# Moving the wait for the last stores from SP, ahead of the closing barriers, to ACT, behind them

## Chip, cores, metric

One core of one Trainium2 chip. Its engines are called PE (TensorE), ACT (ScalarE), DVE (VectorE), POOL (GpSimd) and SP (SyncE). The metric is device microseconds of one execution. Where two kernels are compared, they ran in alternation on the same chip.

## The reference

Max-unpooling: each of 16 x 64 images of 32 x 32 floats is spread over a 64 x 64 image; an index of 0 to 3 says into which of the four places of a 2 x 2 block a value goes, and the other three are zero.

```python
out_i = i * kernel_size + idx // kernel_size
out_j = j * kernel_size + idx % kernel_size
output[b, c, out_i, out_j] = x[b, c, i, j]
```

It reads 4 MB of values and 8 MB of indices (64-bit, of which the low halves are used) and writes 16 MB.

## The kernel before

Three loads are issued ahead of the opening barrier. DVE makes the output in four groups, each from operations "index equals p, times x". SP stores each group, 4 MB, once DVE has made it. The semaphore `stored` counts the last three stores, 16 for each.

```python
class Program:                      # writes the kernel's instructions into the first block
    def __init__(self, nc):
        self.nc = nc
        self.block = nc.main_func.blocks[0]
    ...
        for g in range(NG):         # NG = 4
            nc.sync.wait_ge(made, g + 1)
            nc.sync.dma_start(out=out_v[g], in_=out_t[g]).then_inc(
                stored if g else stored_0, 16
            )
        nc.sync.sem_inc(made, -NG)                                    # L143
        nc.sync.wait_ge(stored, 16 * (NG - 1)).then_inc(stored, -16 * (NG - 1))   # L144
```

Leaving the framework's context (L175) adds the closing code, in a block of its own: a drain of SP, then two barriers of all five engines. (A drain waits for the engine's own work: in this trace DVE's starts at 41.628 us and ends at 55.515, just after DVE's last operation, which ends at 55.467.) In one barrier each of PE, ACT, DVE and SP drains and counts up one semaphore; POOL waits for four counts and releases the four. Behind the program stands what the runtime adds: a chain that each engine has to join, then the clearing of semaphores, then a second chain. In the trace a chain is nine counts of one semaphore; a hop is the time from one count to the next, and an engine's way is the time from the end of its last instruction to its count.

## Time and profile before

| | before |
|---|---|
| time, median of 4 (lowest to highest) | 72.69 us (72.57 to 72.78) |
| span, first to last instruction of the program | 71.00 us |
| last store's last count lands | 70.309 us |
| SP's wait for it is over | 70.343 us |
| last closing instruction (PE) ends | 71.002 us |
| runtime's first chain: first to ninth count | 71.236 to 71.761 us |
| runtime's second chain: ninth count | 72.906 us |

Times inside a run count from the first instruction of the program. "The landing" is the last of the 48 counts of `stored`: with it the last three stores are done. The lower five rows are single records of the trace, which the page does not list: sequencer instructions and the times at which semaphores change. The prediction was written when the kernel before had three runs with a median of 72.71 us.

### The profile page before, as it was taken

What the parts mean: (1) busy time and instruction counts of PE and PEld (TensorE: products, weight loads), DVE (VectorE), ACT (ScalarE), POOL (GpSimd) and SP (SyncE); (2) the same over time, 40 slices, a digit from 0 to 9 for tenths busy, and PEclk for the clock granted to TensorE, in tenths of its full rate; (3) what the DMA queues carried; (4) which work ended last, traced back from release to release, by engine and by line L of the source; (5) the groups of instructions that cost most, each with busy time, mean ns of one, the idle gap of its engine ahead of it and who ended that gap; (6) DMA issues with size and microseconds to landing.
All of it is one profiled execution on the core that took longest, in us unless ns stands there. A gap on an engine that the chain in (4) does not pass through costs nothing.

```text
span 71.0 us, 72 instructions
## 1 busy us (share of the span) xinstructions
DVE 35.6 (50%) x20; POOL 0.2 (0%) x4
## 2 busy tenths in 40 slices
DVE  0000000000089999999999999999999200000000
POOL 1000000000000000000000000000000000000000
DMA  9598997998988999879696989899898979696980
GB/s 277 240 434 378 517 498 314 443 462 378 563 369 369 462 577 438 369 314 572 295 591 295 517 369 517 369 425 462 369 517 351 535 314 572 295 591 295 517 369 0
DMA packets 1009, 29.36 MB, mean 414 GB/s; under 512 B 113, under 2 KB 113, under 8 KB 113
## 3 DMA queue, kind: packets, MB, share of 16 engines
q1 hardware_dynamic: 864, 26.21, 86.4%
q10 hardware_dynamic: 144, 3.15, 10.3%
q14 instruction: 1, 0.00, 0.0%
HBM read 12.58 MB, written 16.78 MB: 414 GB/s over the span
## 4 chain that ended last, share of the span: by engine, by line
DVE 45%; DVEq 4%; issue 1%
DVE out_t L127 45%; DVEq L175 4%
## 5 line engine op out<-in xcount | busy, mean ns | idle before, releaser
L127 DVE SCALAR_TENSOR_TENSOR out_t<-idx_t,x_t 128x2048 f32<-128x2048 int32 (+1 forms) x20 | 35.6, 1860 | 19.9 <-DVEq L116 19.9
L161 POOL MEMSET const-bfloat16-1.0<- 128x1 bf16 x1 | 0.1, 103 | 0.0
L161 POOL MEMSET const-uint8-127<- 128x1 uint8 x1 | 0.1, 102 | 0.0
L161 POOL MEMSET const-float32-1.0<- 128x1 f32 x1 | 0.1, 100 | 0.0
L161 POOL MEMSET const-float32-0.0<- 128x1 f32 x1 | 0.1, 99 | 0.2 <-issue 0.2
## 6 DMA issues: line engine op xcount, KB each, us to landing
out_dram<-out_t SPq DMA_DIRECT2D x4, 4096.0 KB, 13.5
idx_t<-in_indices_dram SPq DMA_DIRECT2D x1, 5120.0 KB, 31.2
x_t<-in_x_dram SPq DMA_DIRECT2D x1, 4096.0 KB, 19.5
idx_t<-in_indices_dram ACTq DMA_DIRECT2D x1, 3072.0 KB, 19.6
```

Of the source, the lines that this page charges most:

```text
L127: op = nc.vector.scalar_tensor_tensor(out=o_c[:, k : k + n, :, pidx // 2, :, pidx % 2], in0=idx_c[:, t : t + n], scalar=pidx, in1=x_c[:, t ...
L161: nc = _bacc.Bacc("TRN2", target_bir_lowering=False, num_devices=1)
L175: with _tile.TileContext(nc) as tc:
```

## The change

Its intent: let the closing barriers run while the stores are still under way, and let one engine alone, ACT, hold up the end until the stores have landed. ACT does nothing else at that time.

```diff
+    def last(self, made):
+        def move(nc):
+            ins = self.block.instructions
+            at = next(k for k, i in enumerate(ins) if i.name == made.ins.name)
+            nc.main_func.blocks[-1].instructions.append(ins.pop(at))
+        self.nc.at_finalize(move)
 ...
         nc.sync.sem_inc(made, -NG)
-        nc.sync.wait_ge(stored, 16 * (NG - 1)).then_inc(stored, -16 * (NG - 1))
+        program.last(
+            nc.scalar.wait_ge(stored, 16 * (NG - 1)).then_inc(stored, -16 * (NG - 1))
+        )
```

`last` takes the instruction out of its place when the program is finished and puts it behind everything else.

## The prediction

> **What bounds the kernel now.** I read the page first, for what was busy to the end; then the chain that ended last; then the SP queue's own waits; then stretches of the tail; and last the single sequencer records of the last microsecond.
>
> ```profile
> span 71.0 us, 72 instructions
> DVE 35.6 (50%) x20; POOL 0.2 (0%) x4
> DVE  0000000000089999999999999999999200000000
> DMA  9598997998988999879696989899898979696980
> HBM read 12.58 MB, written 16.78 MB: 414 GB/s over the span
> out_dram<-out_t SPq DMA_DIRECT2D x4, 4096.0 KB, 13.5
> ```
>
> The DMA row is busy from the first slice to the last but one: 29.36 MB in 71 us. DVE works only in the middle half. So the kernel is bound by its traffic: loads, then four stores of 4 MB. The chain that ended last shows only compute, and so stops early:
>
> ```profile
> 19.79 0.08 issue
> 19.87 11.82 DVE out_t L127 x7
> ...
> 41.63 2.83 DVEq L175
> 44.46 11.01 DVE out_t L127 x5
> ```
>
> It ends at 44.46 + 11.01 = 55.47 us, and 15.5 us of the span are left. (The "DVEq L175" in it is DVE's closing drain, fetched early and held behind its own operations; it is no stop.) What fills the rest is in the SP queue's waits:
>
> ```profile
> SPq L140 <- DVE out_t L127: 53.2, 4, 27.6
> SPq L144 <- SPq L144: 14.5, 1, 14.5
> SPq L175 <- PEq L175: 0.4, 2, 0.3
> ```
>
> L144 is the wait that the change moves. SP sits in it for 14.5 us, until the last three stores have landed. L175 is the closing code, and there are 0.4 us of waits of SP in it. The stretches say what the machine does then:
>
> ```profile
> core 0: us, DVE busy (x) POOL busy (x), PEclk, DMA share, GB/s
> ...
> 55.30:70.30 15.00, 0.17 (x1) 0.00 (x0) 1.00 0.91 393
> 70.30:71.00 0.70, 0.00 (x0) 0.00 (x0) 1.00 0.00 0
> ```
>
> Up to 70.3 us the stores run. In the last 0.7 us no byte moves and no engine computes. That stretch is what the change is about. By the records of the two lines concerned it is all semaphore work:
>
> ```profile
> L144 SPq EVENT_SEMAPHORE  x1: 17/17/17, 70.3 to 70.3; - x1
> ...
> L175 POOLq EVENT_SEMAPHORE  x4: 17/17/17, 70.5 to 70.9; - x4
> L175 SPq DRAIN  x3: 7/7/7, 70.4 to 70.7; - x3
> ...
> L175 ACTq EVENT_SEMAPHORE  x2: 17/17/17, 70.6 to 70.9; - x2
> ...
> L175 PEldq EVENT_SEMAPHORE  x2: 51/51/51, 70.6 to 71.0; - x2
> ```
>
> The single records (us from the span's start): the last 32 KB store packet ends at 69.951; its 16th count lands at 70.309; SP's wait runs 70.326 to 70.343; SP drains at 70.404 and 70.459; POOL sees four arrivals at 70.491 and releases at 70.570; the four others pass at 70.611 to 70.674. A second barrier of the same kind follows: drains from 70.651, PE's the last at 70.774; POOL sees all at 70.819, releases at 70.897; SP, ACT (ends 70.960), DVE and PE pass, PE last, 70.951 to 71.002. From the end of the wait to the end of the span: 71.002 - 70.343 = 0.659 us.
>
> **What the Trainium skill says.** "Perfetto Trace Analysis", section "Summary: the profiler window per engine type": a sequencer instruction is shown for its execution alone, and its wait is hidden. The trace agrees: L144 lasts 17 ns although SP waited 14.5 us. "DMA: Bandwidth & Descriptors", section on the anatomy of one DMA: a semaphore is only counted up once the last byte is confirmed. Here the last count comes 70.309 - 69.951 = 0.36 us after the last data packet. The change keeps that. "Runtime: NRT & Kernel Launch", section "The ~15µs preamble/postamble breakdown": behind the program stands the runtime's own barrier of all engines, a chain over five engines with some 44 ns a hop, then the clearing of semaphores, then another barrier. The trace has them: nine counts of one semaphore at 71.236, 71.271, 71.476, 71.520, 71.543, 71.641, 71.681, 71.715 and 71.761; clears of semaphores from 71.661 to 72.325; nine counts more, 72.549 to 72.906. So hops are 23 to 98 ns here, but one took 205 ns.
>
> **The change, part by part.**
> (1) Removed: SP's wait ahead of its closing drain. SP's last other work, taking `made` back, ends at 55.89. SP then reaches the closing barriers at once. DVE's drain ended at 55.515 and ACT, PE and POOL have been there since 1.3 us. So both barriers run at about 55.9 to 56.6, under the stores, some 13.7 us before they can matter. Their 0.659 us leave the path.
> (2) Added: the same wait as the last instruction of ACT, behind both barriers. The list of the built program confirms it: ACT's wait for 48 is the very last instruction; nothing else moves (the comparison of instruction orders shows shifted line numbers only). Cost: 17 ns on ACT as on SP, since every event instruction of ACT and SP is 17 ns. So ACT ends at 70.34, and I expect a **span of 70.34 us**.
> (3) Unmoved: issues, DVE's work and transfers. The stores land at 70.31 as before.
> (4) Behind the span: the runtime's barrier used to start once all five had come out of the second closing barrier, PE last at 71.002. Now four engines stand in it for 14 us and only ACT is missing. Which place ACT has in the chain the trace does not name. If it is second (its count at 71.271, 0.311 after its own end at 70.960), the second count comes at 70.343 plus at most 0.311, thus by 70.654, and the rest goes at the pace of the undisturbed opening chain, where the seven hops from the second count to the ninth took 38+43+24+112+39+34+46 = 336 ns: over by 70.99 instead of 71.761, a gain of at least 0.77. With only 0.1 us for ACT's way there it would be 0.98. If ACT is the third, the late one, its way is 71.476 - 70.960 = 0.516 and the gain 71.761 - (70.343 + 0.516 + 0.298) = 0.60; as fifth (count at 71.543, way at most 0.583, then 0.231) at least 0.60. Reading the clears by their blocks of numbers, I take the order to be PE, ACT, POOL, DVE, SP: ACT second. The late third is then POOL, which has long been there after the change.
> Sum: 0.659 from the span, plus about 0.15 of the runtime's chain that is waited out earlier: **some 0.8 us**. The profiled run took 72.79 for a span of 71.00, so the metric holds 1.79 us beside the span, and I take it that the first runtime barrier is inside that. 72.71 - 0.8 = **71.9 us**, 1.1% less.
>
> **The rivals.**
> (a) **Span only.** The runtime's part does not shrink, or it is outside the metric: 72.71 - 0.66 = 72.05. For it: 1.79 us beside the span are not itemised by any view. Against: the late hop of 205 ns is waiting, and can be hidden.
> (b) **Nothing gained.** Whatever the metric ends on waits for something other than the five engines, for example a slower way out of ACT after a long wait, or work in the closing that POOL or SP does only once stores are done: 72.7. For it: on several engines the way from the last instruction to the runtime's chain is up to 0.5 us, and unseen. Against: that way was paid before too, after the barriers.
> (c) **The whole tail goes**, and with it more of the runtime's closing: engines that came early might clear their semaphores under the stores. That would save 1.5 us or more: 71.2. Against: the clears start only at 71.661, after the chain has turned round, hence after all arrivals; ACT's missing arrival holds them as before.
> (d) **Slower.** Four engines waiting early could disturb the stores. They move nothing, and SP waited through the same 14.5 us before. Cost 0.
>
> **Range and chances.** The centre is 71.9. The places of ACT in the chain span 0.60 to 0.98, thus 71.73 to 72.11; the runs of before scatter from 72.57 to 72.78, so a median may be off by 0.1. That gives 71.65 to 72.2, with (a) inside and (b) and (c) outside. Faster by over 2% needs a gain of 1.45 us, twice what stands behind the wait: 0.03. Slower by 2% has no mechanism: 0.01. Within 2%: 0.96.
>
> **What will show it.** Right: a span near 70.3; closing-code records (L187) of SP, POOL, DVE and PE near 56 us and none after 57; ACT's event for the stores at 70.3 as the last of all; the stores' landing still about 14.8 us after the last issue; the runtime's chain over by about 71.0 and the clears in the same shape some 0.8 us sooner. Step (2) is wrong if ACT's event lasts much over 17 ns or comes much later than the last count; step (4) is wrong if the profiled time falls by just the span's 0.66, or by less. The whole is wrong if the last store lands later, or if the closing barriers still stand at the end.

## The result

| | time, median (lowest to highest) | ratio to before |
|---|---|---|
| before | 72.69 us (72.57 to 72.78), 4 runs | |
| changed | 71.83 us (71.83 to 71.85), 4 runs | 0.9883 (0.9866 to 0.9901) |

A ratio is the mean time of one kernel's runs over that of the other's of the same rounds, so it is not quite the ratio of the medians quoted; the interval is of 95%. The change gains 1.2%: clear of noise.

The page of the changed kernel:

```profile
span 70.3 us, 72 instructions
DMA  9699998999988899969999896979999997969792
HBM read 12.58 MB, written 16.78 MB: 417 GB/s over the span
```

The traffic is the same, the span is 0.7 us shorter, and the DMA row no longer ends in an idle slice. The chain that ended last still stops with DVE (start, length, what):

```profile
44.37 11.01 DVE out_t L137 x5
```

55.38 us, against 55.47 before: the work was not touched. The SP queue's waits (total, times, longest):

```profile
SPq L150 <- DVE out_t L137: 53.1, 4, 27.5
SPq L187 <- PEq L187: 0.4, 2, 0.3
```

The wait of 14.5 us has gone from SP, while the 0.4 us in the closing code, now L187, are still there. They have moved in time, as the records of the closing code say (durations in ns, then first and last start in us):

```profile
L187 POOLq EVENT_SEMAPHORE  x4: 17/17/17, 56.0 to 56.4; - x4
L187 SPq DRAIN  x3: 7/7/64, 55.9 to 56.2; - x3
...
L187 PEldq EVENT_SEMAPHORE  x2: 51/51/51, 56.1 to 56.5; - x2
```

Before, these stood at 70.4 to 71.0 us. The barriers are as long as they were, but run under the stores. And the moved wait:

```profile
L155 ACTq EVENT_SEMAPHORE  x1: 17/17/17, 70.3 to 70.3; - x1
```

It is the only instruction of the program after 56.6 us. The stretches show the same end:

```profile
55.30:70.30 15.00, 0.08 (x1) 0.00 (x0) 1.00 0.91 393
70.30:70.40 0.10, 0.00 (x0) 0.00 (x0) 1.00 0.00 0
```

The stores run at 393 GB/s in both kernels; barriers and engines waiting beside them do not slow them. What comes after the span is seen in the nine counts of the runtime's first chain (single records, us from the span's start):

```
               landed   1      2      3      4      5      6      7      8      9
before         70.309 71.236 71.271 71.476 71.520 71.543 71.641 71.681 71.715 71.761
changed        70.291 56.755 70.474 70.512 70.555 70.579 70.678 70.716 70.750 70.797
```

In the changed kernel the first count comes at 56.755, 0.234 us after the closing barriers are over, and the second is held for 13.7 us. One engine stands ahead of ACT in the chain, so ACT is the second. The third count follows 38 ns later, not 205. From the landing to the ninth count it takes 70.797 - 70.291 = 0.506 us, against 71.761 - 70.309 = 1.452 before: 0.946 us less. From there to the ninth count of the second chain it is 1.145 and 1.148 us: unchanged. The two profiled runs took 72.79 and 71.83 us, 0.96 apart. The metric thus moves with the runtime's chain, not with the span, which fell by 0.673.

### The profile page after: what moved, and what is told of

Read it like the earlier page. It is cut to its first block, busy times and chain, and to the rows that moved or that the text cites. A ratio compares the mean times of both kernels' runs of the same rounds, so it can differ in the third digit from the quotient of the medians.

```text
span 70.3 us, 72 instructions
## 1 busy us (share of the span) xinstructions
DVE 35.6 (51%) x20; POOL 0.2 (0%) x4
## 4 chain that ended last, share of the span: by engine, by line
DVE 46%; DVEq 4%; issue 1%
DVE out_t L137 46%; DVEq L187 4%
```

## The experiments

One theory and its rivals were left after this. **T:** what counts is the work that still stands between the landing and the ninth count: closing barriers, the engine's way into the chain, and the hops behind its place. **Rivals:** the gain needs ACT in place of SP (E); the place in the chain does not matter (P); barriers cost wherever they stand. Eleven runs, all correct, on three chips. The last column is read from each profiled run, in us.

| run | who waits, and where | median us | ratio to before (95%) | landing to ninth count |
|---|---|---|---|---|
| e1 | ACT, behind both barriers (the change) | 71.71 | 0.9863 (0.9848 to 0.9878) | 0.506 |
| e2 | ACT, ahead of both | 72.65 | 0.9991 (0.9978 to 1.0005) | 1.417 |
| e3 | SP, behind both | 71.55 | 0.9843 (0.9828 to 0.9858) | 0.332 |
| e4 | POOL, behind both | 72.16 | 0.9925 (0.9912 to 0.9938) | 0.887 |
| e5 | SP, between them | 72.34 | 0.9946 (0.9932 to 0.9959) | 1.065 |
| e6 | SP, ahead of three barriers | 73.03 | 1.0038 (1.0025 to 1.0051) | 1.780 |
| e7 | ACT, behind three barriers | 71.71 | 0.9853 (0.9840 to 0.9867) | 0.505 |
| e8 | PE, behind both | 71.95 | 0.9887 (0.9874 to 0.9901) | 0.712 |
| e9 | DVE, behind both | 71.71 | 0.9861 (0.9847 to 0.9876) | 0.473 |
| e10 | SP, behind both, again | 71.59 | 0.9844 (0.9830 to 0.9858) | 0.332 |
| e11 | ACT, behind both, again | 71.72 | 0.9864 (0.9850 to 0.9878) | 0.507 |

The kernel before had 72.68, 72.75 and 72.74 us (e1 to e4, e5 to e8, e9 to e11).

### e1: the changed kernel as yardstick

No edit.

> The changed kernel once more, as the yardstick of this chip for the three that follow. Theory T (what counts is what still stands behind the last store: the 0.66 us of closing barriers have gone under the stores, and the runtime's chain is entered by its second engine, ACT, with 0.47 us left to its ninth count): 71.83 us, 0.85 us under the kernel before; closing-code records near 56 us; the ninth count of the runtime's chain near 70.80. Every rival expects the same here.

71.71 us and 0.9863: a little more gain than at first (0.9883). The trace after the landing is the same to the nanosecond, 0.506 us; the landing itself was earlier, 70.077. The two profiled runs took 71.83 and 71.61 us: 0.22 apart, as their landings are (0.214). So the difference between these two is when the transfers were over, and nothing behind them.

### e2: ACT waits, but where SP did

```diff
-        nc.sync.wait_ge(stored, 16 * (NG - 1)).then_inc(stored, -16 * (NG - 1))
+        nc.scalar.wait_ge(stored, 16 * (NG - 1)).then_inc(stored, -16 * (NG - 1))
```

> ACT waits instead of SP, but ahead of the closing barriers, where SP's wait was. Theory T: both barriers are behind the stores again, so the time is that of the kernel before, 72.69, or at most 0.06 less, as ACT has one closing drain behind its wait where SP has two (61 ns between them in the trace of before). Span near 70.95. Rival E (ACT is the better engine to wait on, wherever it waits): near 71.8.

0.9991, an interval that holds 1. Rival E falls: the engine alone is worth nothing that the time shows. The SP queue's wait tells where the 14.5 us went, with the records of ACT's drains below it:

```profile
SPq L175 <- PEq L175: 14.9, 2, 14.6
```

```profile
L175 ACTq DRAIN  x2: 8/8/8, 70.3 to 70.6; - x2
```

SP now stands in the first closing barrier for 14.6 us, because ACT's drain for it comes at 70.3 and no longer at 1.3 us. (The view names PE as the releaser; the one that came last is ACT.) Landing to ninth count is 1.417 us, 0.035 less than before; I had allowed up to 0.06 for SP's second drain. (The 61 ns of the expectation lie between the end of SP's wait and its first drain; the two drains start 55 ns apart.)

### e3: SP waits, behind the barriers

The edit, against the changed kernel:

```diff
-            nc.scalar.wait_ge(stored, 16 * (NG - 1)).then_inc(stored, -16 * (NG - 1))
+            nc.sync.wait_ge(stored, 16 * (NG - 1)).then_inc(stored, -16 * (NG - 1))
```

> SP keeps the wait, but behind the closing barriers. Theory T with the order PE, ACT, POOL, DVE, SP in the runtime's chain: SP is the turning point, so four counts are in long before and only the fifth to ninth (0.218 us after the fifth) are behind the stores; if SP needs 0.145 us from its last instruction to its count as ACT did, the ninth count is 0.36 us after the wait against ACT's 0.468: 71.73 us. Four counts near 56.8 to 57.1. Rival E (the gain needs ACT): near 72.7. Rival P (the place in the chain does not matter): 71.83.

71.55 us, where 71.73 was expected: the place alone gives the whole gain, and 0.16 us more than ACT's in the medians. In the SP queue's waits the long one is back, and the end is early all the same:

```profile
SPq L155 <- SPq L155: 13.9, 1, 13.9
SPq L187 <- PEq L187: 0.4, 2, 0.3
```

The counts of e3, e4, e8 and e9 together show where each engine stands:

```
               landed   1      2      3      4      5      6      7      8      9
e3 SP          70.160 56.611 56.645 56.850 56.895 70.328 70.372 70.410 70.445 70.492
e4 POOL        70.305 56.778 56.812 70.907 70.950 70.974 71.071 71.111 71.145 71.192
e8 PE          70.283 70.637 70.671 70.709 70.753 70.777 70.875 70.914 70.948 70.995
e9 DVE         70.145 56.628 56.662 56.867 70.376 70.400 70.498 70.537 70.571 70.618
```

With SP four counts are in before the landing, and the fifth is held. With SP as the last to come the sixth count follows the fifth in 44 ns; in the other runs that hop takes 97 to 99. This I had not expected (0.363 us from SP's wait against 0.298 measured, 70.492 - 70.194). Why it is shorter no run here shows. (One reading, untested: in all other runs the sixth count comes 121 to 123 ns after the fourth, which is DVE's by row e9; with SP last the fourth count is 13.4 us old by then. If the sixth were DVE's again, DVE might need that time between its two counts.)

### e4: POOL waits, behind the barriers

The same edit with `nc.gpsimd`.

> POOL waits, behind the closing barriers. In the kernel before, the third count of the runtime's chain came 205 ns after the second instead of 38; I take the third to be POOL and that it needs 0.56 us from its last instruction (70.914) to its count (71.476). Theory T: third count 0.56 us after POOL's wait and 0.285 more to the ninth, 0.85 us after the wait against ACT's 0.468: 72.2 us. If the third is not POOL or its way is as short as ACT's 0.145: 71.79. Rival P (place and engine do not matter): 71.83.

72.16 us, as theory T had it. The third count comes 70.907 - 70.346 = 0.561 us after POOL's last instruction. In the kernel before it was 71.476 - 70.914 = 0.562. So POOL is the third of the chain, and its long way was what made the third hop 205 ns. In the changed kernel it must be over long before ACT's count; in e3 and e9, where the third count is not held up, it comes at 56.850 and 56.867 us. Rival P falls: the same change with another engine keeps about half the gain.

### e5: SP waits between the two barriers

```diff
-            nc.main_func.blocks[-1].instructions.append(ins.pop(at))
+            end = nc.main_func.blocks[-1].instructions
+            moved = ins.pop(at)
+            mine = [k for k, i in enumerate(end)
+                    if i.engine == moved.engine and isinstance(i, mybir.InstDrain)]
+            end.insert(mine[-1], moved)
 ...
-            nc.scalar.wait_ge(stored, ...
+            nc.sync.wait_ge(stored, ...
```

> SP waits between the two closing barriers: the first is under the stores, the second behind them. Theory T (each closing barrier that stands behind the stores costs its own time): the second takes 0.329 us from PE's exit of the first to PE's exit of the second in the trace of before; of the part before it one SP drain (0.06) less. From the wait's end to PE's exit some 0.28 us instead of 0.659: 72.31 us. Closing-code records both near 56 us and near 70.4. Rival (only the order against the very last barrier counts, the gain is all or nothing): 72.7 or 71.8.

72.34 us. One barrier ran early, one late, as POOL's records say (first and last start):

```profile
L194 POOLq EVENT_SEMAPHORE  x4: 17/17/17, 56.0 to 70.4; - x4
```

The gain is not all or nothing: landing to ninth count fell by 1.452 - 1.065 = 0.387 us for the one barrier and one SP drain, and POOL's long way is late again (third hop 205 ns).

### e6: a third barrier behind the wait

Against the kernel before:

```diff
     with _tile.TileContext(nc) as tc:
         tile_max_unpool_kernel(tc, *args)
+    nc.all_engine_barrier()
```

> The kernel before with a third closing barrier behind its two. Theory T: one more of 0.329 us behind the stores: 73.02 us, span 71.33. Rival (the barriers are cheap, the gain of the change came from the runtime's chain): 72.7.

73.03 us. The added barrier's records:

```profile
L177 SPq DRAIN  x1: 7/7/7, 71.0 to 71.0; - x1
...
L177 PEldq EVENT_SEMAPHORE  x1: 51/51/51, 71.2 to 71.2; - x1
```

Landing to ninth count grew by 1.780 - 1.452 = 0.328 us, and the median of the same chip by 73.03 - 72.75 = 0.28. The cost of one closing barrier behind the stores is thus measured by adding one (0.328), and e5 agrees by taking one away.

### e7: the same third barrier, ahead of ACT's wait

The same added line, in the changed kernel.

> The changed kernel with a third closing barrier, ahead of ACT's wait. Theory T: the third barrier runs near 56.5 to 56.9 us, under the stores, and costs nothing: the time of the changed kernel, 71.7 to 71.85. Rival (barriers cost wherever they are, for example by disturbing the stores): 72.0 to 72.2.

71.71 us. The same barrier stands under the stores:

```profile
L189 SPq DRAIN  x1: 7/7/7, 56.4 to 56.4; - x1
...
L189 PEldq EVENT_SEMAPHORE  x1: 51/51/51, 56.6 to 56.6; - x1
```

It costs nothing: landing to ninth count 0.505 us against 0.506. e6 and e7 are the plainest pair: one barrier, two places, 0.33 us or none.

### e8: PE waits, behind the barriers

The same edit as e3 with `nc.tensor`.

> PE waits, behind the closing barriers. Theory T: PE is the first of the runtime's chain and slow, an event takes it 51 ns and its way to its count 0.234 us; then eight hops of 0.359. From the last landing to the ninth count 0.017 + 0.051 + 0.234 + 0.359 = 0.66 us against 0.506 with ACT: 0.155 over the changed kernel, about 71.9 to 72.0. No count of the runtime's chain before the stores have landed. Rival P (place and engine do not matter): the time of the changed kernel.

71.95 us. No count of the chain precedes the landing: PE is the first. Its way from the end of its wait to its count is 70.637 - 70.362 = 0.275 us, where the kernel before had 0.234; I had used 0.234, and so expected 0.66 us from the landing to the ninth count where 0.712 came.

### e9: DVE waits, behind the barriers

The same edit with `nc.vector`.

> DVE waits, behind the closing barriers. Theory T with DVE the fourth in the runtime's chain: three counts near 56.6 to 57.0, the fourth to ninth behind the stores. DVE's way to its count is not known (under 0.549 us in the trace of before); scaled from SP's 0.134 by the 21 and 17 ns of an event it is about 0.165; the hops from the fourth count take 0.242. From the last landing to the ninth count 0.017 + 0.021 + 0.165 + 0.242 = 0.445 us, between SP's 0.332 and ACT's 0.506: some 0.06 under the changed kernel, about 71.65. Rival P (place does not matter): as the changed kernel.

DVE is the fourth, as supposed. From the landing to the ninth count 0.473 us, where I expected 0.445: its way is 0.183 us and not 0.165. Against ACT's 0.507 that should be 0.03 us in the time; 71.71 against 71.72 us (0.9861 and 0.9864) can't tell that from nothing.

### e10 and e11: SP against ACT on one chip, again

No edit beyond those of e3 and e1.

> SP waits, behind the closing barriers, once more, to compare it with ACT on the same chip. Theory T: landing to ninth count 0.332 us as in the first run of it, 0.17 less than with ACT; time 0.1 to 0.2 us under the changed kernel of the same rounds. If the first difference was the scatter of the landings alone: the same time as ACT.

> The changed kernel, as the yardstick of these rounds: 0.985 to 0.989 of the kernel before; landing to ninth count 0.506 us.

0.9844 and 0.9864, on another chip than e3 and e1 with their 0.9843 and 0.9863. Landing to ninth count was 0.332 and 0.507 us again. The intervals overlap, but both chips show the same difference, and the trace has 0.17 us for it. So SP behind the barriers is the fastest version seen: 1.6% under the kernel before.

### All runs together

If theory T is the whole of it, the median less "landing to ninth count" must be one constant. Over all thirteen profiled runs it is 71.20 to 71.32 us: 72.69 - 1.452 = 71.24 before, 71.83 - 0.506 = 71.32 for the first reading of the change, 71.71 - 0.506 = 71.20 in e1, 72.16 - 0.887 = 71.27 with POOL, 73.03 - 1.780 = 71.25 with three barriers. The times themselves differ by 1.5 us. What is left, 0.12 us, has no pattern with barriers, engine or place.

This compares medians with the trace of one run each. Inside the profiled runs it is sharper: the run's own time less the time of its ninth count is 1.024 to 1.034 us in all thirteen (72.79 - 71.761 = 1.029 before, 71.83 - 70.797 = 1.033 changed, 71.52 - 70.492 = 1.028 in e3). So up to 0.01 us, to which the times are given, a run's time is its ninth count and a constant; what is left above is when the stores landed, 70.077 to 70.309 us in these runs.

## Why the prediction was right

It gave 71.9 us, 71.65 to 72.2, and "within 2%" at 0.96; measured were 71.83 us at first and 71.71 and 71.72 in later rounds. The range also held rival (a), 72.05, so the time alone would not have told the two apart; the traces do. That the first reading came within 0.1 us is in part luck: the sum was too small by 0.15 us (part 4), and the first two medians lie 0.86 us apart where the traces have 0.946 and later rounds 0.97 and 1.02.

**Part 1, barriers under the stores:** right. They ran from 55.9 to 56.52 us (foretold 55.9 to 56.6), and their 0.659 us left the path; e5, e6 and e7 show the price and that it is nil under the stores.

**Part 2, the wait on ACT costs 17 ns and the span becomes 70.34:** right, 17 ns and 70.33.

**Part 3, transfers unmoved:** right. 393 GB/s in the last stretch in both, the landing at 70.291 against 70.309.

**Part 4, the runtime's chain:** right in mechanism, small in size. The order PE, ACT, POOL, DVE, SP was read from the clears of semaphores and is now shown by e1, e3, e4, e8 and e9. (The prediction does not show that reading of the clears, only what came of it.) The chain was foretold to be over by about 71.0 and is over at 70.797; the clears start at 70.696 instead of 71.661, 0.97 us sooner and not 0.8. For the sum took 0.15 us for this part, and the trace has 0.29: from the end of the last instruction to the ninth count it took 71.761 - 71.002 = 0.759 us before and 70.797 - 70.329 = 0.468 after. Of that difference POOL's late count is 205 - 38 = 167 ns. The other 124 ns are PE's way and one hop (0.234 + 0.035 = 0.269) against ACT's own way (70.474 - 70.329 = 0.145). The prediction had the span of 0.77 to 0.98 for ACT as second and then mixed in the other places; with the order that it believed, and the 0.1 that it tried for ACT's way, it would have said 0.98; with the way of 0.145 that ACT turned out to have, 0.94. The trace shows 0.946. The term that was mis-sized is thus the chain's. One remark in the range is off too: 1.45 us is not twice what stands behind the wait, since barriers and chain together are 0.659 + 0.759 = 1.418 us.

**Rivals.** (a), the span only, falls: 0.946 on the trace against 0.673 of span. (b), nothing gained, falls, though POOL's way of 0.56 us, unseen in the page, was real and is what e4 pays. (c), earlier clears, did not come about: after the chain 1.148 us follow, as 1.145 did before. (d): e7 shows that barriers beside the stores do not slow them.

## What to carry to other kernels

In this kernel the wait for the last stores did best behind everything else that has to be done once: the closing work then runs under the transfer, and the other engines have already arrived when the last byte lands. Which engine holds the wait matters by tenths of a microsecond: here SP was the cheapest (0.33 us from landing to the ninth count) and POOL the dearest (0.89), so try it rather than take the idle one. This is worth 1.2 to 1.6% of a kernel of 73 us. By the traces it saves 0.95 us with ACT and 1.12 with SP. If that is the same in a longer kernel with the same closing code, the share is smaller there; no run here shows another kernel.

## What the Trainium skill lacked or had wrong

- "Runtime: NRT & Kernel Launch", "The ~15µs preamble/postamble breakdown", has the chain over five engines at 44 ns a hop times 8, in its row for the barrier ahead of the program. The sum agrees nearly (370 ns from the first to the ninth count of the chain ahead of the program, 357 for the second chain behind it, both before the change), the single hops do not: 23, 34, 38, 39, 45, 46 and one of 98 ns behind the program, each place having its own.
- The same section does not give the order or what it means for who should arrive last. The runs show PE, ACT, POOL, DVE, SP for the first five counts, and from the landing to the ninth count 0.71, 0.51, 0.89, 0.47 and 0.33 us when that engine holds the last wait. Whose the last four counts are no run shows.
- No page has the way from an engine's last instruction to its count in that chain: ACT 0.145 us, SP 0.134, DVE 0.183, PE 0.234 to 0.279, POOL 0.56. What POOL does in it no run shows.
- "Runtime: NRT & Kernel Launch", the same section, puts the clearing of semaphores behind the program at about 1.5 us; here the clears went from 71.661 to 72.325 us before the change, 0.66 us over all engines.
- "DMA: Bandwidth & Descriptors", "Anatomy of one DMA — SWDGE (gpsimd) path", gives the receipt most of some 2 us on that path. It has no such time for SP's queue, by which these stores went: the last count came 0.33 to 0.40 us after the end of the last data packet. No run here isolates the rest of the fixed cost.
